# A hybrid encoder block: a fourth g_attn unit in the state-space rounds, side work at fixed places in an attention block

## The chip, the cores and the metric

The kernel runs on one core of one Trainium2 chip. The core has TensorE (PE, matmuls), VectorE (DVE), ScalarE (ACT), GpSimd (POOL) and SyncE (SP), which here only issues DMAs. Each engine executes its own instructions in the order in which the program issues them and waits on semaphores for the others. The metric is the device time of one execution in microseconds (us).

## The reference

One layer of an encoder block on a sequence of 1024 tokens of width 1024, in float32:

```python
proj = h @ w_in                     # h = RMSNorm(x) * (1 + scale) + shift
q, k, v, z_a, u, z_s, g_a, g_s = jnp.split(proj, IN_OFFSETS, axis=-1)
o = diff_attention(rope(q), rope(k), v, lam)          # 4 heads, two softmax maps each
o = rmsnorm(o, g_subln) * (1.0 - lam_init)            # per head
attn_branch = (o.reshape(b, s, ATTN_WIDTH) * jax.nn.silu(z_a)) @ w_up_attn
y = s5_forward(u) + s5_backward(u) + d_skip * u       # 32 groups, complex diagonal state
y = jax.nn.gelu(y); y = y * jax.nn.sigmoid(y @ w_glu + b_glu)
ssm_branch = (y * jax.nn.silu(z_s)) @ w_up_ssm
merged = jax.nn.sigmoid(g_a) * attn_branch + jax.nn.sigmoid(g_s) * ssm_branch
out = rmsnorm(x + gate * (merged @ w_out), g_final)
```

The projection's 128 column blocks that matter here: eight blocks of g_attn (g_a), whose tanh is kept in DRAM until the merge.

## The kernel before

Every float32 product is made of three matmuls: a weight is split into a high part `wh` (ACT copies it into a rounded type) and a low part `wl` (DVE or POOL subtracts), the other operand likewise, and high times high, high times low and low times high are summed in PSUM. A *unit* (`unit`, lines 209 to 222) is 128 columns of the projection: two halves of 512 tokens, eight steps of three matmuls each, so 16 steps. Weights come in the order of the list `plan`; `w_ahead` (called in the first step of a unit) loads and splits those of the next unit or two. `w_state["eng"]` says whether DVE or POOL makes the low parts: DVE in the state-space rounds, POOL in attention.

The program is a hand-made order. A *main* generator issues the work of a stage and yields amounts of budget; `drive` takes that budget from a *fill* generator, whose units yield 0.66 per step. So the constants `YF, YA, YB, YC` (state-space rounds, `ssm_main`) and `FA, FB, LA, LB` (attention, `s3_main`) say how many fill steps stand between the pieces of main work on PE.

- State-space rounds (`ssm_main`): eight rounds; in each DVE does the stages a, rot, c, s (scans) and d. Four yields of YA, one of YB and one of YC a round. The fill is the rest of u, z_ssm, z_attn, g_ssm and the first `GA1 = 3` units of g_attn.
- `s2_main`: what is left of that fill, then the gated linear unit and the up-projection of the state-space branch (`unit_pair`, evacuated by `up_ev` on DVE as tile `pt`).
- Attention (`s3_main`): 34 blocks g, eight per head. A block issues `qk` (scores; DVE takes the maximum, ACT the exponential), `mix` of the block before (the DVE operation on tile `e`), `pv` in odd blocks, half of the fill, the other half, `transpose_w` of the block before (PE transposes of `e`; ACT and DVE split them into `wth` and `wtl`), and the late fill. `spot(0)`, `spot(1)` and `spot(2)` are three places in it for side work. The fill is q, k and v of heads 1 to 3 and the remaining units of g_attn.
- Side work: the rope of q and k (`turn`: a shuffle on DVE and three operations on POOL; `cut`: the split, ACT and POOL) waits in the queue `pend` and `with_pend` pops one entry at every second fill step, wherever in a block that is. `make_v` and, right behind it, `o_turn` (PE transposes of the last head's output) stand in block 2 of a head; the steps of `o_norm` (the head's RMSNorm) stand at every spot after that, one each.
- `s3_tail`: the turn and the norm of head 3, reloads of the normed heads, splits into `oh` and `ol`, under what is left of the fill; then the up-projection of attention, the merge and the output projection.

Of the kernel before, what the change touches and what calls it, by code (L numbers as in the profile page):

```python
# [9 lines left out]
F32 = mybir.dt.float32  # L10
# [56 lines left out]
def tile_hybrid_block(  # L67
# [63 lines left out]
    w0 = w_in[0]  # L131
    OQ, OK, OV, OZA, OU, OZS, OGA, OGS = 0, 512, 1024, 1536, 2048, 2560, 3072, 4096

    GA1 = 3
    YF, YA, YB, YC, YL = 10.5, 2.6, 4.6, 2.8, 3.0
    NPE = (3, 4, 2, 1, 0, 0, 0, 1)
    WN = 16
    plan = []
# [39 lines left out]
    def w_split():  # L178
        i = w_state["split"]
        if i >= len(plan):  # L180
            return
        r = w_raw.pop(i)
        h = pp.tile([P, 8 * P], F32R, tag="wh", bufs=2, name="wh")
        l = pp.tile([P, 8 * P], F32R, tag="wl", bufs=2, name="wl")
        split(h, l, r, w_state["eng"])
        k = plan[i][2]
        w_hl[i] = tuple(t[:].rearrange("p (k n) -> p k n", k=k) for t in (h, l))
        w_state["split"] += 1
# [17 lines left out]
        while w_state["load"] <= min(i + 1, len(plan) - 1):  # L206
            w_load()

    def unit(c0, K, rh, rl, evac, pool=None, w=None, off=0, ahead=True):
        wh, wl = w or w_get(c0)  # L210
        for hf in range(2):
            ps = (pool or ps_mm).tile([P, 512], F32, tag="mm", name="mm")
            sl = slice(hf * 512, hf * 512 + 512)
            n = 0
            for k in range(K):
                for a, r in ((wh, rh), (wh, rl), (wl, rh)):
                    PE.matmul(out=ps, lhsT=a[:, k, off:off + P], rhs=r[:, k, sl], start=(n == 0), stop=(n == 3 * K - 1))  # L217
                    n += 1
                if ahead and hf == 0 and k == 0:
                    w_ahead()  # L220
                yield 0.66
            evac(hf, sl, ps)

    def unit_pair(c0, rh, rl, evacs, pool=None):
        w = w_get(c0)
        for b in range(2):
            yield from unit(c0, 4, rh, rl, evacs[b], pool, w, b * P, b == 0)

    def run_all(g):
        for _ in g:  # L230
# [964 lines left out]
    def s2_main():  # L1195
        ps2 = tc.alloc_tile_pool(name="ps_s2", bufs=1, space=PSUM, side="right")
        yp = tc.alloc_tile_pool(name="yp", bufs=1, side="right")
        y2h = yp.tile([P, 4, S], F32R, name="y2h")
        y2l = yp.tile([P, 4, S], F32R, name="y2l")
        gts = {}  # L1200

        def load_g(m):
            if m < 8:
                gts[m] = yp.tile([P, S], F32, tag="gt", bufs=3, name="gt")
                SP.dma_start(out=gts[m], in_=gsd[m])

        yq = tc.alloc_tile_pool(name="yq", bufs=1, side="right")
        yh = yq.tile([P, 4, S], F32R, name="yh")
        yl = yq.tile([P, 4, S], F32R, name="yl")
        zts = {}  # L1210

        def load_z(n):
            if n < 4:
                zts[n] = yq.tile([P, S], F32, tag="zt", bufs=2, name="zt")
                SP.dma_start(out=zts[n], in_=zsd[n])

        co = yp.tile([P, T * 8], F32, name="cos")
        sn = yp.tile([P, T * 8], F32, name="sin")
        yp.tile([P, 120], F32, name="pad")
        G.tensor_copy(out=co, in_=rt["co"])  # L1220
        G.tensor_copy(out=sn, in_=rt["sn"])
        rt.update(co=co, sn=sn)
        t = yq.tile([P, S], F32, name="yt")
        for r in range(2):
            SP.dma_start(out=t[64 * r:64 * r + 64], in_=yd[3 * P + 64 * r:3 * P + 64 * r + 64, :])
        yield 2.0
        for b in range(3):
            split(yh[:, b], yl[:, b], ye[:, b])
            yield 1.5
        load_z(0)  # L1230
        load_z(1)
        act(t[0:64], t[0:64], AF.Gelu_apprx_tanh)
        split(yh[:, 3], yl[:, 3], t)
        yield 1000.0

        def glu_ev(n):
            def ev(hf, sl, ps):
                zt = zts[n]
                sg = yq.tile([P, 512], F32, tag="sg", bufs=2, name="sg")
                mul(zt[:, sl], zt[:, sl], (ye[:, n] if n < 3 else t)[:, sl])  # L1240
                act(sg, ps, AF.Sigmoid, bias=cols[:, CBG + n:CBG + n + 1])
                mul(sg, sg, zt[:, sl])
                split(y2h[:, n, sl], y2l[:, n, sl], sg)
                if hf == 1:
                    load_z(n + 2)
            return ev

        for n in range(0, 4, 2):
            for q in unit_pair(n * P, yh, yl, [glu_ev(n), glu_ev(n + 1)]):
                yield q  # L1250
            if n == 0:
                for m in range(3):
                    load_g(m)
        yq.release()
        yep.release()
        p2 = tc.alloc_tile_pool(name="p2", bufs=1, side="left")
        cosT = p2.tile([P, S], F32, name="cosT")
        sinT = p2.tile([P, S], F32, name="sinT")
        rt.update(p2=p2, cosT=cosT, sinT=sinT)
        yg = tc.alloc_tile_pool(name="yg", bufs=1, side="right")  # L1260
        prep = side_prep(yg, ps2)
        pts = {}
        def up_ev(m):
            def ev(hf, sl, ps):
                gt = gts[m]
                if hf == 0:
                    pts[m] = yg.tile([P, S], F32, tag="pt", bufs=2, name="pt")
                stt(pts[m][:, sl], gt[:, sl], 1.0, ps, ALU.add, ALU.mult)
                if hf == 1:
                    A.dma_start(out=pad[m], in_=pts[m])  # L1270
                    load_g(m + 3)
            return ev

        for m in range(0, 8, 2):
            for q in unit_pair(m * P, y2h, y2l, [up_ev(m), up_ev(m + 1)]):
                next(prep, None)
                yield q
        run_all(prep)
        yg.release()
        yp.release()  # L1280
        ps2.release()
# [17 lines left out]

    def skip():  # L1300
        pass

    def with_pend(g, every):
        for n, q in enumerate(g):
# [4 lines left out]
    def rope_unit(c0, scale, h, finish):  # L1309
        t = {}  # L1310

        def ev(hf, sl, ps):
# [21 lines left out]
                if h == 0:  # L1334
                    finish(hi, lo, sl)

            pend.extend([turn, skip, skip, cut])
            if hf == 1 and h > 0:
                pend.append(lambda: finish(t["h"], lo, slice(0, S)))
        yield from unit(c0, 8, hh, hl, ev)  # L1340

    def prep_q(h):
# [67 lines left out]
    def qk(g):  # L1410
        h, i = divmod(g, 8)
        H = heads[h]
        if i == 0:
            flush()
            H["o"] = po.tile([P, S], F32, tag="o", bufs=2, name="o")
            H["zr"] = po.tile([P, 8, 2], F32, tag="zr", bufs=2, name="zr")
        tok = slice(i * P, i * P + P)
# [64 lines left out]
    def o_norm(h, e=G, big=None):  # L1482
        H = heads[h]
        on, zr, o = H["on"], H["zr"], H["o"]
        ss = po.tile([P, 8], F32, tag="oss", name="oss")
        z2 = po.tile([P, 8], F32, tag="wm", bufs=2, name="z2")
        for hf in range(2):
            sl = slice(hf * 512, hf * 512 + 512)
            if big is None:
                jk = p3.tile([P, 512], F32, tag="tb", name="sq")  # L1490
            else:
                jk = big[:, sl]
            act(jk, o[:, sl], AF.Square)
            yield
            V.tensor_reduce(out=ss[:, 4 * hf:4 * hf + 4], in_=jk.rearrange("p (t e) -> p t e", t=4) if big is not None
                            else jk[:].rearrange("p (t e) -> p t e", t=4), axis=AX.X, op=ALU.add)
        mul(z2, zr[:, :, 0], zr[:, :, 0])
        mul(ss, ss, z2)
        yield
        res = []  # L1500
        for n, _ in enumerate(rsqrt_gen(po, ss, 8, 1.0 / P, "o", res)):
            if n % 3 == 2:
                yield
        rs = res[0]
        mul(rs, rs, zr[:, :, 0])
        mul(on, on, bc(rs[:], 2, [P, 8, P]), e)
        yield
# [15 lines left out]
    def s3_main():  # L1523
# [4 lines left out]
        NG = 32  # L1528
        gens = {}

        def spot(s, g):
            h, i = divmod(g, 8)
            if g < 8:
                return
            if (i, s) == (2, 0) and h < 4:
                make_v(h)
            if (i, s) == (2, 1) and h < 4:
                o_turn(h - 1)
                gens[h] = o_norm(h - 1)
            elif h in gens and next(gens[h], gens) is gens:  # L1540
                gens.pop(h)
            if (i, s) == (5, 0):
                load_za(h - 1)
            if (i, s) == (6, 0):
                assert h not in gens
                SP.dma_start(out=ofd[h - 1], in_=o_back(h - 1))

        for g in range(NG + 2):
            fa, fb = (FA, FB) if g < 24 else (LA, LB)
# [15 lines left out]
            spot(2, g)  # L1565
            yield fb / 2

    FA, FB, FD = 3.1, 1.0, 1.0
    LA, LB = 2.45, 1.0
    fill3 = with_pend(s3_fill(), 2)  # L1570
    drive(s3_main(), fill3)
    p3.release()
    p2.release()
# [12 lines left out]
    def s3_tail():  # L1586
# [5 lines left out]
        for h in range(3):  # L1592
            ofl.append(op.tile([P, S], F32, tag="sg", bufs=3, name="ofl"))
            SP.dma_start(out=ofl[h], in_=ofd[h])
        next(norm)
        yield 3.0
        run_all(norm)
# [195 lines left out]
```

## Time and profile before

| | us |
|---|---|
| median of 3 runs (lowest to highest) | 912.46 (911.06 to 912.81) |
| the profiled execution | 911.19 |
| its span, first to last instruction | 909.3 |
| PE busy in the span | 873.0 |
| rounds with their fill | about 108 to 340 |
| attention | 459 to 754 |
| norm tail | 754 to 769.5 |

The times of the rows come from the one profiled execution, counted from the start of its span. A matmul's end is modelled and matmuls overlap, so the idle time of PE is taken from stretches and from the starts of matmuls, not from the sum of durations.

### The profile page before, as it was taken

The page shows a single profiled execution, that of the slowest core. Times are in us where ns is not written, and L with a number is a line of the kernel's source. Part 1 is how long each engine was busy: PE and PEld are TensorE (multiplying, and loading weights), DVE is VectorE, ACT ScalarE, POOL GpSimd, SP SyncE. Part 2 cuts the span into 40 slices and gives each one's busy share as a digit, 9 for nine tenths or more (in the row PEclk, how much of TensorE's full clock was granted, in tenths as well). Part 3 has the DMA queues.
Part 4 walks back from the last instruction along what each step waited for, and adds up shares of the span by engine and source line. Part 5 has one row for each costly group of instructions (what it writes and reads, how often), then busy time and mean ns, then how long its engine had stood idle before and what let it go on. Part 6 is the DMA issues. An engine that isn't in the chain of part 4 may idle for free.

```text
span 909.3 us, 12201 instructions
## 1 busy us (share of the span) xinstructions
PE 873.0 (96%) x4528; PEld 732.6 (81%) x4528; DVE 673.3 (74%) x1264; ACT 366.1 (40%) x610; POOL 134.5 (15%) x115
## 2 busy tenths in 40 slices
PE   5999999999999899999999999898999999999996
PEld 4878888888888788787878887787788888887886
DVE  5986999899999976674657767875866756573465
ACT  6754442132222236301246556455555544232222
POOL 1001000000000001000025434423511111350000
PEclk9899899999999999999999999999999999999999
DMA  9936133333243446595433313132232224848022
GB/s 296 307 83 186 52 112 110 101 98 118 85 126 107 125 139 196 207 327 185 123 98 81 91 38 81 64 95 63 70 105 58 81 94 140 333 176 312 12 88 98
DMA packets 107117, 119.56 MB, mean 131 GB/s; under 512 B 7716, under 2 KB 87825, under 8 KB 107059
## 3 DMA queue, kind: packets, MB, share of 16 engines
q1 hardware_dynamic: 105268, 114.08, 40.5%
q10 hardware_dynamic: 1614, 4.51, 1.2%
q8 instruction: 36, 0.59, 0.3%
q0 software_dynamic: 176, 0.20, 0.1%
q14 instruction: 23, 0.18, 0.1%
HBM read 78.46 MB, written 27.73 MB: 117 GB/s over the span
## 4 chain that ended last, share of the span: by engine, by line
PE 41%; DVE 7%; ACT 3%; DMA 2%; issue 2%; POOL 2%; SPq 0%; ACTq 0%; DVEq 0%; POOLq 0%
PE mm L217 19%; PE op L1712 9%; PE pv L1468 4%; PE tp L1457 3%; PE sc L1427 3%; PE sc L1426 2%; DVE nm L1428 2%; POOL pta L78 1%; DVE e L96 1%; ACT e L99 1%; DVE wtl L78 1%; DMA wor<-in_w_out_dram 1%; DMA pad<-pt 1%; ACT mh L99 1%; DMA pta<-pad 1%
## 5 line engine op out<-in xcount | busy, mean ns | idle before, releaser
L217 PE MATMUL mm<-hh,wh 128*128 128x512 f32 x592 | 239.1, 404 | 0.0
L217 PE MATMUL mm<-hh,wl 128*128 128x512 f32 x592 | 232.6, 393 | 2.9 <-DVE wl L78 2.8
L217 PE MATMUL mm<-hl,wh 128*128 128x512 f32 x592 | 232.6, 393 | 0.0
L217 PEld LDWEIGHTS mm<-hh,wl 128*128 128x128 f32 x592 | 112.1, 189 | 28.2 <-DVE wl L78 4.1
L217 PEld LDWEIGHTS mm<-hh,wh 128*128 128x128 f32 x592 | 112.3, 190 | 22.4 <-issue 1.7
L217 PEld LDWEIGHTS mm<-hl,wh 128*128 128x128 f32 x592 | 112.5, 190 | 20.4
L99 ACT ACTIVATE e<-sc,nm 128x1024 f32<-128x1024 f32 x64 | 71.2, 1115 | 77.1 <-DVE nm L1428 77.0
L1428 DVE TENSOR_REDUCE nm<-sc 128x1 f32<-128x1024 f32 x64 | 75.3, 1218 | 14.2 <-PE sc L1427 13.1
L78 DVE TENSOR_TENSOR wtl<-tp,wth 128x512 fp32r<-128x512 f32 x64 | 41.2, 686 | 60.0 <-ACT wth L99 59.9
L99 ACT ACTIVATE wh<-wr 128x1024 fp32r<-128x1024 f32 x49 | 51.7, 1056 | 62.0 <-DMA wr<-in_w_in_dram 24.2
L99 ACT ACTIVATE side<-mm 128x512 f32<-128x512 f32 x48 | 28.7, 598 | 112.8 <-PE mm L217 78.5
L78 POOL TENSOR_TENSOR wl<-wr,wh 128x1024 fp32r<-128x1024 f32 x14 | 34.7, 2477 | 207.2 <-ACT wh L99 207.0
L78 DVE TENSOR_TENSOR wl<-wr,wh 128x1024 fp32r<-128x1024 f32 x35 | 42.9, 1227 | 29.2 <-ACT wh L99 29.0
L1712 PE MATMUL op<-woh,ml 128*128 128x512 f32 (+1 forms) x136 | 51.3, 377 | 1.1 <-DVE ml L78 1.1
L1712 PE MATMUL op<-wol,mh 128*128 128x512 f32 (+1 forms) x136 | 51.2, 377 | 0.0
L1712 PE MATMUL op<-woh,mh 128*128 128x512 f32 (+1 forms) x136 | 51.2, 377 | 0.0
L99 ACT ACTIVATE wth<-tp 128x512 fp32r<-128x512 f32 x64 | 34.8, 596 | 40.1 <-PE tp L1457 40.1
L1426 PE MATMUL sc<-kk,qq 128*128 128x512 f32 x128 | 49.9, 390 | 0.0
L1427 PE MATMUL sc<-kk,qb 128*128 128x512 f32 x128 | 49.9, 390 | 0.0
L96 DVE SCALAR_TENSOR_TENSOR e<-e,wm 128x1024 f32<-128x1024 f32 x32 | 45.3, 1415 | 1.1
L1468 PE MATMUL pv<-wth,vh 128*128 128x256 f32 x128 | 36.5, 285 | 2.7 <-DVE wtl L78 2.7
L1457 PE MATMUL tp<-cst,e 128*128 128x128 f32 x256 | 33.3, 273 | 5.8 <-DVE nry L78 2.4
(365 smaller groups left out, 1693.1 us busy)
## 6 DMA issues: line engine op xcount, KB each, us to landing
wr<-in_w_in_dram SPq DMA_DIRECT2D x40, 512.0 KB
wa<-in_w_ada_dram SPq DMA_DIRECT2D x16, 512.0 KB
x<-in_x_dram SPq DMA_DIRECT2D x8, 512.0 KB
gsd<-side SPq DMA_DIRECT2D x8, 512.0 KB
gad<-side SPq DMA_DIRECT2D x8, 512.0 KB
gt<-gsd SPq DMA_DIRECT2D x8, 512.0 KB
wg<-in_w_ada_dram SPq DMA_DIRECT2D x8, 512.0 KB
pad<-pt ACTq DMA_DIRECT2D x8, 512.0 KB
```

Of the source, the lines that this page charges most:

```text
L78: (e or V).tensor_tensor(out=o, in0=a, in1=b, op=op)
L96: V.scalar_tensor_tensor(out=o, in0=a, scalar=s, in1=b, op0=op0, op1=op1)
L99: A.activation(out=o, in_=i, func=f, **kw)
L217: PE.matmul(out=ps, lhsT=a[:, k, off:off + P], rhs=r[:, k, sl], start=(n == 0), stop=(n == 3 * K - 1))
L1426: PE.matmul(out=sc[:, sl], lhsT=H["qq"][:, cc, tok], rhs=H["kk"][:, cc, sl], start=True, stop=False)
L1427: PE.matmul(out=sc[:, sl], lhsT=qb_t[g // 2][:, cc, tb], rhs=H["kk"][:, cc, sl], start=False, stop=True)
L1428: V.tensor_reduce(out=nm[:, cc:cc + 1], in_=sc, axis=AX.X, op=ALU.max, negate=True)
L1457: PE.transpose(ps[:, k, :], e[:, kt * P:kt * P + P], ident)
L1468: PE.matmul(out=ps[:, 0:256], lhsT=a[:, kt, :], rhs=r[:, kt, :], start=(n == 0), stop=(n == 23))
L1712: PE.matmul(out=ps[:, 0:n], lhsT=a[:, k, tok], rhs=r[:, k, lo:lo + n], start=(i == 0), stop=(i == 23))
```

## The change

It puts a fourth unit of g_attn into the rounds (`GA1`), with larger Y constants; raises `FA` from 3.1 to 3.2; cuts POOL's subtraction for a weight split into two halves; lets `unit_pair` of the state-space up-projection call `w_ahead` at the second half's first step; and gives each kind of side work a place: turns at spot 0 of a block, one each; the last cut of a head at spot 2 from block 5 on; `o_turn` at block 3, spot 1; the nine steps of `o_norm` at the places of `STEPS`; the transposes back and the store of a normed head at block 0 of the head after next.

```diff
-    GA1 = 3
-    YF, YA, YB, YC, YL = 10.5, 2.6, 4.6, 2.8, 3.0
+    GA1 = 4
+    YF, YA, YB, YC, YL = 12.0, 2.75, 4.8, 3.2, 3.0
...
-        split(h, l, r, w_state["eng"])
+        act(h, r, AF.Copy)
+        if w_state["eng"] is G:
+            for j in range(0, 8 * P, 512):
+                sub(l[:, j:j + 512], r[:, j:j + 512], f32(h[:, j:j + 512]), G)
+        else:
+            sub(l, r, f32(h))
...
-                if ahead and hf == 0 and k == 0:
+                if (hf, k) == ahead:
                     w_ahead()
...
-            for q in unit_pair(m * P, y2h, y2l, [up_ev(m), up_ev(m + 1)]):
+            for q in unit_pair(m * P, y2h, y2l, [up_ev(m), up_ev(m + 1)], ahead=(1, 0)):
...
+    def pop_turn():
+        while pend:
+            kind, fn = pend.popleft()
+            fn()
+            if kind == "turn":
+                break
+
+    def pop_cut():
+        if pend and pend[0][0] == "cut":
+            pend.popleft()[1]()
...
-            pend.extend([turn, skip, skip, cut])
-            if hf == 1 and h > 0:
-                pend.append(lambda: finish(t["h"], lo, slice(0, S)))
+            def cut_all():
+                cut()
+                if hf == 1:
+                    finish(t["h"], lo, slice(0, S))
+
+            pend.extend([turn, skip, skip, cut] if h == 0 else [("turn", turn), ("cut", cut_all)])
...
         if i == 0:
-            flush()
+            while pend:
+                pop_turn()
...
             act(jk, o[:, sl], AF.Square)
             yield
+            if hf == 1:
+                z2 = po.tile([P, 8], F32, tag="wm", bufs=2, name="z2")
             V.tensor_reduce(out=ss[:, 4 * hf:4 * hf + 4], in_=jk.rearrange("p (t e) -> p t e", t=4) if big is not None
                             else jk[:].rearrange("p (t e) -> p t e", t=4), axis=AX.X, op=ALU.add)
+            if hf == 0:
+                yield
...
+        STEPS = ((3, 2), (4, 0), (4, 2), (5, 0), (5, 1), (6, 0), (6, 1), (7, 0), (7, 1))
+
         def spot(s, g):
             h, i = divmod(g, 8)
-            if g < 8:
+            if 1 <= h < 4 and (i, s) in STEPS:
+                next(gens[h], None)
+            if s == 0:
+                pop_turn()
+            if s == 2 and i >= 5:
+                pop_cut()
+            if (i, s) == (0, 0) and h >= 2:
+                SP.dma_start(out=ofd[h - 2], in_=o_back(h - 2))
+            if not 1 <= h < 4:
                 return
-            if (i, s) == (2, 0) and h < 4:
+            if (i, s) == (2, 0):
                 make_v(h)
-            if (i, s) == (2, 1) and h < 4:
+            if (i, s) == (3, 1):
                 o_turn(h - 1)
                 gens[h] = o_norm(h - 1)
-            elif h in gens and next(gens[h], gens) is gens:
-                gens.pop(h)
-            if (i, s) == (5, 0):
+            if (i, s) == (7, 0):
                 load_za(h - 1)
-            if (i, s) == (6, 0):
-                assert h not in gens
-                SP.dma_start(out=ofd[h - 1], in_=o_back(h - 1))
...
-    FA, FB, FD = 3.1, 1.0, 1.0
+    FA, FB, FD = 3.2, 1.0, 1.0
     LA, LB = 2.45, 1.0
-    fill3 = with_pend(s3_fill(), 2)
+    fill3 = s3_fill()
...
         next(norm)
+        next(norm)
         yield 3.0
```

## Rows read from the trace of the kernel before

**Rows 1.** Page, part 1: busy us (share of the span) xinstructions
```profile
PE 873.0 (96%) x4528; PEld 732.6 (81%) x4528; DVE 673.3 (74%) x1264; ACT 366.1 (40%) x610; POOL 134.5 (15%) x115
```

**Rows 2.** Chain of waits in order of time: start us, us, what
```profile
754.07 12.94 PE mm L217 x57
```

**Rows 3.** Waits, PE: engine line waited for: us in total, times, longest us
```profile
PE tp L1479 <- DVE vl L78: 3.2, 3, 1.1
PE mm L217 <- DVE wl L78: 2.8, 1, 2.8
PE pv L1468 <- DVE wtl L78: 2.7, 3, 2.0
PE tp L1457 <- DVE nry L78: 2.4, 2, 1.7
PE tp L1457 <- DVE nrt L78: 2.2, 2, 1.3
PE mm L217 <- DVE pt L96: 1.3, 1, 1.3
```

**Rows 4.** Stretches: length, busy us of PE, PEld, DVE, ACT, POOL, granted clock, DMA
```profile
203.40:228.20 24.80, 24.80 (x147) 21.21 (x147) 24.13 (x36) 6.78 (x13) 0.20 (x2) 1.00 0.42 125
302.80:327.00 24.20, 21.38 (x121) 17.80 (x120) 23.17 (x33) 3.85 (x9) 0.20 (x2) 0.93 0.29 86
459.00:541.00 82.00, 80.62 (x438) 69.26 (x439) 56.23 (x76) 46.07 (x81) 34.12 (x23) 1.00 0.29 75
541.00:616.00 75.00, 70.51 (x398) 60.06 (x397) 56.46 (x85) 39.70 (x72) 30.79 (x21) 1.00 0.29 78
616.00:691.00 75.00, 70.23 (x396) 59.67 (x395) 52.97 (x84) 39.43 (x72) 24.33 (x16) 1.00 0.26 71
691.00:754.00 63.00, 61.66 (x360) 53.20 (x360) 41.10 (x70) 32.71 (x59) 9.13 (x4) 1.00 0.29 94
754.00:769.50 15.50, 15.50 (x74) 12.93 (x73) 11.96 (x23) 7.36 (x11) 3.40 (x1) 1.00 0.33 113
...
313.00:316.00 3.00, 3.00 (x9) 2.33 (x8) 2.93 (x7) 0.00 (x0) 0.00 (x0) 0.50 0.00 0
```

**Rows 5.** Timeline, the late weight split: start us, us, engine line op tiles
```profile
300.02 1.06 ACT L99 ACTIVATE wh<-wr 128x1024 fp32r<-128x1024 f32 x1 [6.11 <-DMA wr<-in_w_in_dram]
...
310.79 1.23 DVE L78 TENSOR_TENSOR wl<-wr,wh 128x1024 fp32r<-128x1024 f32 x1
```

**Rows 6.** Timeline of DVE at the first state-space up-projection
```profile
380.60 1.23 DVE L78 TENSOR_TENSOR wl<-wr,wh 128x1024 fp32r<-128x1024 f32 x1 [0.26 <-ACT wh L99]
381.74 1.28 DVE L96 SCALAR_TENSOR_TENSOR pt<-gt,mm 128x512 f32<-128x512 f32 x2
```

**Rows 7.** Timeline of DVE and POOL in two attention blocks
```profile
566.27 2.40 DVE L96 SCALAR_TENSOR_TENSOR e<-e,wm 128x1024 f32<-128x1024 f32 x1
...
566.30 1.29 POOL L78 TENSOR_TENSOR rq<-rq,rs 128x512 f32<-128x512 f32 x1
568.58 2.43 POOL L78 TENSOR_TENSOR wl<-wr,wh 128x1024 fp32r<-128x1024 f32 x1 [0.99 <-ACT wh L99]
...
603.93 1.28 DVE L96 SCALAR_TENSOR_TENSOR e<-e,wm 128x1024 f32<-128x1024 f32 x1
```

**Rows 8.** Timeline of PE, DVE and ACT in the norm tail
```profile
753.03 1.03 PE L1479 MATMUL tp<-cst,o 128*128 128x128 f32 x8
...
759.74 1.23 DVE L78 TENSOR_TENSOR o<-o,nry 128x1024 f32<-128x1024 f32 x1
760.88 5.69 DVE L78 TENSOR_TENSOR ol<-ofl,oh 128x1024 fp32r<-128x1024 f32 x3
767.48 1.41 DVE L96 SCALAR_TENSOR_TENSOR of<-tp,cols,of 128x512 f32<-128x512 f32 x2 [0.91 <-PE tp L1516]
...
768.92 1.06 ACT L99 ACTIVATE oh<-of 128x1024 fp32r<-128x1024 f32 x1 [4.63 <-DVE of L96]
770.02 1.23 DVE L78 TENSOR_TENSOR ol<-of,oh 128x1024 fp32r<-128x1024 f32 x1 [1.13 <-ACT oh L99]
```

More of the change, by code (lines that the diff above doesn't have):

```diff
@@ L207, in w_ahead, with unit @@
             w_load()
-    def unit(c0, K, rh, rl, evac, pool=None, w=None, off=0, ahead=True):
+    def unit(c0, K, rh, rl, evac, pool=None, w=None, off=0, ahead=(0, 0)):
         wh, wl = w or w_get(c0)
@@ L222, in unit, with unit_pair @@
             evac(hf, sl, ps)
-    def unit_pair(c0, rh, rl, evacs, pool=None):
+    def unit_pair(c0, rh, rl, evacs, pool=None, ahead=(0, 0)):
         w = w_get(c0)
         for b in range(2):
-            yield from unit(c0, 4, rh, rl, evacs[b], pool, w, b * P, b == 0)
+            yield from unit(c0, 4, rh, rl, evacs[b], pool, w, b * P, None if b else ahead)
     def run_all(g):
@@ L1485, in o_norm @@
         ss = po.tile([P, 8], F32, tag="oss", name="oss")
-        z2 = po.tile([P, 8], F32, tag="wm", bufs=2, name="z2")
         for hf in range(2):
```

## Prediction

> **What bounds the kernel now.** I read the page first: TensorE (PE) is busy 96% of the span, VectorE (DVE) 74%, GpSimd (POOL) 15% [rows 1]. PE executes in order, so the time is PE's work plus PE's gaps, and an edit is worth the gaps that it closes or opens. PE's work is not changed by this edit: the same matmuls run. 57 matmuls of 512 columns take 12.94 us in the chain of waits [rows 2], 0.227 us each; one unit of 48 is 10.9 us, one fill step (three matmuls) 0.68 us.
>
> Next the list of waits, PE's own [rows 3]: six entries carry the inner gaps. The stretches say where they lie [rows 4]. In attention (459 to 754 us) PE is busy 80.62 of 82, 70.51 of 75, 70.23 of 75 and 61.66 of 63 us: 12.0 us of gaps, 9.3 of them in the two middle rows, the blocks of heads 1 and 2, where rope work for the next head and the norm of the last head meet. In a state-space round (203.4 to 228.2) PE is busy 24.80 of 24.80 and DVE 24.13: both are full, and DVE is about to be the later one. At the end of the rounds it is: between 302.8 and 327 PE is idle for 2.8 us and the granted clock is 0.93, another 0.07 x 24.2 = 1.7 us. In the norm tail (754 to 769.5) PE is busy throughout.
>
> **The change, part by part.**
>
> *One unit moves (GA1 = 4, the Y values).* The rounds' budget grows by 1.5 + 8 x (4 x 0.15 + 0.2 + 0.4) = 11.1, that is 16.8 steps of 0.66, and the unit has 16. So the rounds take the whole unit, +10.9 us of PE there, and attention loses 10.9. Net of work: nothing. What the rounds gain is slack for DVE: 1.2 of budget more a round, 1.24 us of PE time, while DVE gets one weight split more in all. At 308.9 the matmul that waited needed a weight low part whose high part ScalarE (ACT) had ready at 301.08; DVE started it at 310.79 [rows 5], 9.7 us late, behind a backlog. With 0.7 us a round DVE was nearly level; with 1.9 us over eight rounds the backlog goes. I take the whole gap and the clock dip behind it away: **-4.5 us**. Bounds: 0 (another split falls behind the scans) to -4.5. The fill that is left after the last round, which covers the prologue of the gate, shrinks by at most one step; the stretch from 327 to 354 has no gap and I cost this at nothing; without that cover it would be up to 0.7.
>
> *Split of the up-projection's weights one half later (ahead = (1, 0)).* At 380.73 PE waits for DVE to clear a PSUM half. DVE did the weight split (380.60, 1.23 us) ahead of the clearing operation pt [rows 6]. In the new order pt comes first and the wait of 1.3 us [rows 3] goes: **-1.3**. The split is now 2.7 us later in a pair that lasts 10.9 us, so its reader is not late; bounds -1.3 to 0.
>
> *Side work at fixed places in attention.* (a) The turn of the head's output (o_turn) moves from right behind make_v to the next block. In all three heads PE waited 1.1 us for vl, whose PSUM buffers it needed [rows 3]: 3.2 us, gone; at the new place the buffers were cleared a block before. (b) The norm steps and the rope turns: PE's transposes wait for nrt and nry (4.6 us) and pv for wtl (2.7 us) [rows 3]. The rows show why. The mixing operation e takes 1.28 us at 603.93 but 2.40 at 566.27, where POOL runs a rope addition of 1.29 from 566.30 [rows 7]: the longer by what POOL took. So a DVE operation with two SBUF inputs stands still beside POOL. In the new order the rope work starts right behind e in each block (spot 0) and has most of a block (295 us / 34 = 8.7) until the next e: cut 1.3 + turn 3 x 1.3 = 5.2 us of POOL [rows 7], so it is over by then unless a weight split (2.43 us [rows 7], now two halves) falls in. And only one norm step stands in front of a transpose instead of a varying number. Of the 12.0 us I leave 2.5: the first block's wait and the last pv's, which nothing here touches (about 1.2), and one or two collisions of 1.3. **-9.5**, bounds -11 (only the untouched waits stay) and -4 (only the 3.2 of o_turn and one more go). Neither (a) nor (b) adds PE work.
> The Trainium skill (GPSIMD Engine Reference, section 1, Specifications) says that GpSimd's SBUF interfaces are shared with VectorE and contend with its two-input instructions; the rows above agree, and by that rule alone a POOL chain that runs into the next e costs again what it cost before, which is the second rival.
>
> *Moved DMAs and queues.* The store of a normed head moves from block 6 to block 0 of the head after, the load of za from block 5 to 7. On SyncE's queue the weight loads and query copies behind the store wait for the same few DVE operations as before, and have a unit's time (10.9 us) of lead; for head 2 the store falls into block 32, some 5 us before its reload is issued, which waits for pv's end in any case. I cost them at nothing; a load that is late would cost 1 to 2 us. The halved POOL split adds 0.1 us per split on an engine that is busy 15%.
>
> *Fill 4.2.* Counting steps by the budget rule: 24 blocks and 10 late blocks used 202 of 224 steps before, and 22 were left for the tail; now they use 205 of 208, and **3 are left**. This is the price of the change. The norm of head 3 ran under 19 steps of fill. Its chain [rows 8]: from the turn at 753.03 to the multiply by the norm at 759.74 is 6.7 us; then 1.23 for it, 3 x 1.23 for the low parts of heads 0 to 2 (they took 5.69 because POOL was splitting beside them; that split is now earlier), 1.41 for `of`, 1.06 for the high part and 1.23 for the low part: 15.3 us. PE has in that time two turns of 1.03, nine fill matmuls (2.04) and ten of the up-projection that need not wait for head 3 (2.27): 6.4. So PE idles **+9.0 us**, where it had no gap. Bounds: 7 (part of the small operations overlap) to 10.5 (the slow low parts return).
>
> *The clock behind that gap.* After the 2.8 us gap at 309 the granted clock was 0.50 from 313 to 316 [rows 4], half of full, that is 1.2 instead of 2.4 GHz: 1.5 us lost. The new gap is longer. I take **+1.5**, bounds 0 (it comes back before the up-projection runs densely) and 3 (twice as long low).
> The Trainium skill (TensorE: Matmul & The Clock Gate, "Why this matters for your kernels") warns against idle gaps in the middle of a kernel because the clock falls; it speaks against this part, and row and rule agree on the sign.
>
> **Sum.** -4.5 - 1.3 - 9.5 + 9.0 + 1.5 = -4.8. The profiled execution took 911.19 (span 909.3 and 1.9 around it), the median of the runs is 912.46, so the profile is 1.3 us under the median. From the profile 906.4, from the median 907.7; I say **907.0**.
>
> **The rivals.**
> 1. *Forecast*, 904.5 to 910: chance 0.52.
> 2. *Slower: the POOL chain still runs into e.* Each of the 12 blocks with a rope turn loses 1.1 us (2.40 - 1.28), so the 12.0 us of gaps stay, while the tail pays its 10.5. 911.19 - 4.5 - 1.3 + 10.5 = 915.9, from the median 917. It decides as soon as fewer than 4.7 of the 12.0 us go. For it: ACT must make the cut's high part behind two exponentials before POOL can begin, so the chain ends late in the block. Against it: the blocks from 459 to 541 already had such turns and lost only 1.4 us. Chance 0.13.
> 3. *The waits only half go* (about 6 of 12.0): 911.19 - 4.5 - 1.3 - 6 + 10.5 = 909.9, from the median 911: 0.15, at the edge of the 0.2% bound, so I split it evenly between faster and same.
> 4. *The rounds stay bound by DVE*, so that the unit is moved but the gap at 309 stays or moves: 906.4 + 4.5 = 910.9, from the median 912. DVE is over 97% busy in a round, but the added fill is three to four times what it needs: 0.08.
> 5. *The tail is cheaper* (7 us, no clock loss) and attention loses only 1 us: 911.19 - 4.5 - 1.3 - 11 + 7 = 901.4, from the median 902.7: 0.12.
>
> **How the numbers follow.** Faster by over 0.2% (1.8 us, about what measurement can tell from no change) means under 910.6: the forecast, rival 5 and half of rival 3, 0.71. Within it: rival 4, half of 3 and a little of 2, 0.17. Slower: 0.12. The range 902.5 to 913.5 takes in the bounds of the tail and of the attention waits and leaves out most of rival 2 and the best end of rival 5.
>
> **What would show it.** In the profile after: rounds of about 26.0 us with PE full, DVE under 24.5, and no gap for wl at their end, granted clock 1.00; no wait for pt at the first up-projection of the state-space branch; no waits for vl in o_turn, and 1 to 4 us of gaps over all attention blocks; between the last pv and the first up-projection of attention a gap of 8 to 10 us on PE that ends on DVE's ol, with a granted clock near 0.5 in or behind it; every e near 1.28 us. The prediction is wrong in its first term if that tail gap is under 6 us, and in its main gain if e still shows 2.4 in many blocks.

## The result, and the profile after

| | us |
|---|---|
| before, median of 4 runs (lowest to highest) | 912.62 (911.06 to 912.81) |
| after, median of 4 runs (lowest to highest) | 901.87 (899.86 to 902.09) |
| ratio, with its 95% interval | 0.9885 (0.9871 to 0.9900) |
| the profiled execution of after; its span | 901.95; 899.7 |

The changed kernel is faster, by 10.7 us where 5.5 were forecast. The time lies 0.6 us under the lower end of the range.

The waits of PE in the profile after (engine, line, what it waited for: us in total, times, longest us), those of the lead-in left out, are the counterpart of [rows 3]:

```profile
PE tp L1539 <- DVE o L78: 4.9, 1, 4.9
PE mm L222 <- DVE of L96: 2.8, 1, 2.8
PE tp L1477 <- DVE nrt L78: 1.2, 1, 1.2
PE tp L1539 <- POOL wl L78: 0.7, 1, 0.7
```

Of the six entries of [rows 3], five are gone (vl, wl, wtl, nry, pt) and nrt went from 2.2 to 1.2 us. New are the two on `o` and `of`, 7.7 us, both in the norm of head 3, and one of 0.7 us on POOL's `wl`.

The stretches of the profile after (length, busy us of PE, PEld, DVE, ACT, POOL, granted clock, DMA share, GB/s) answer to [rows 4]: a round, the last rounds, the four parts of attention, the norm tail, and the half of the tail behind its first gap:

```profile
208.00:234.20 26.20, 26.20 (x153) 22.38 (x153) 24.60 (x37) 7.14 (x13) 0.20 (x2) 1.00 0.41 123
312.00:338.00 26.00, 26.00 (x150) 22.10 (x149) 19.90 (x31) 8.09 (x14) 0.20 (x2) 1.00 0.50 146
...
463.00:545.00 82.00, 81.52 (x442) 70.05 (x443) 54.51 (x75) 45.57 (x79) 33.14 (x27) 1.00 0.30 78
545.00:620.00 75.00, 73.77 (x418) 63.73 (x418) 57.26 (x89) 41.97 (x76) 32.92 (x26) 1.00 0.29 78
620.00:695.00 75.00, 75.00 (x427) 65.01 (x426) 55.97 (x91) 44.74 (x80) 26.86 (x21) 1.00 0.31 85
695.00:745.00 50.00, 49.30 (x292) 42.68 (x291) 34.54 (x60) 25.35 (x45) 6.92 (x5) 1.00 0.21 70
745.00:764.00 19.00, 11.30 (x49) 9.06 (x48) 12.01 (x25) 8.17 (x11) 0.00 (x0) 0.73 0.70 252
...
756.00:764.00 8.00, 5.21 (x17) 4.08 (x16) 6.39 (x7) 2.00 (x2) 0.00 (x0) 0.53 0.80 270
```

PE is full through the rounds, DVE has 1.6 us to spare in one, and the end of the rounds has neither its gap nor its clock of 0.93. Attention shows 2.4 us of idle PE (0.48 + 1.23 + 0 + 0.70) where it had 12.0. In the tail PE is busy 11.3 of 19 us, and the granted clock falls to 0.53, near the lower of its two levels (1.2 of 2.4 GHz).

**PE's lost time by stage.** Idle time between modelled ends is not the whole of what PE loses. The next table goes by the starts of matmuls alone: between each two successive starts, what is over the 0.227 us of a 512 column matmul (or the usual step of a shorter one), added up by stage. These sums are worked out from all matmul starts of each profile, and with the number of matmuls in a stage they give its length. For the profile after they come to 9.7 us less than before; its span is 9.6 us shorter (909.3 to 899.7).

| lost time, us | before | after | a_ga3 | b_unit | g_waste | w2 |
|---|---|---|---|---|---|---|
| lead-in, up to the first stage c | 19.0 | 18.6 | 20.1 | 18.4 | 18.4 | 20.1 |
| rounds | 5.6 | 0.6 | 5.8 | 0.6 | 0.6 | 0.6 |
| up-projection of the state-space branch | 4.4 | 2.3 | 2.3 | 4.4 | 2.3 | 2.8 |
| attention blocks, to the last pv | 18.8 | 7.4 | 7.0 | 18.9 | 7.0 | 6.8 |
| norm tail | 0.2 | 9.1 | 1.5 | 7.1 | 1.4 | 1.5 |
| up-projection of attention | -0.1 | 1.7 | 0.1 | 2.6 | 0.1 | 0.1 |
| output projection and end | 1.3 | -0.1 | 1.6 | -0.1 | -0.1 | 1.5 |

(The other columns belong to the experiments; g_waste has in its tail 34 extra matmuls, 7.7 us of work, that are not lost time.)

### The profile page after: what moved, and what is told of

It reads as the page before. It is cut to its first block, busy times and chain, and to the rows that moved or that the text cites. A ratio compares the mean times of both kernels' runs of the same rounds, so it can differ in the third digit from the quotient of the medians.

```text
span 899.7 us, 12212 instructions
## 1 busy us (share of the span) xinstructions
PE 870.5 (97%) x4528; PEld 734.0 (82%) x4528; DVE 667.8 (74%) x1265; ACT 366.3 (41%) x610; POOL 132.9 (15%) x127
## 5 line engine op out<-in xcount | busy, mean ns | idle before, releaser
L222 PE MATMUL mm<-hh,wh 128*128 128x512 f32 x592 | 238.2, 402 | 0.0
L222 PE MATMUL mm<-hl,wh 128*128 128x512 f32 x592 | 232.0, 392 | 0.0
L222 PE MATMUL mm<-hh,wl 128*128 128x512 f32 x592 | 231.7, 391 | 0.0
L222 PEld LDWEIGHTS mm<-hh,wl 128*128 128x128 f32 x592 | 111.7, 189 | 24.3 <-DVE wl L78 0.5
L222 PEld LDWEIGHTS mm<-hh,wh 128*128 128x128 f32 x592 | 111.9, 189 | 22.4 <-issue 1.7
L222 PEld LDWEIGHTS mm<-hl,wh 128*128 128x128 f32 x592 | 112.0, 189 | 20.2
L78 DVE TENSOR_TENSOR wtl<-tp,wth 128x512 fp32r<-128x512 f32 x64 | 41.2, 686 | 55.7 <-ACT wth L99 55.7
L78 DVE TENSOR_TENSOR wl<-wr,wh 128x1024 fp32r<-128x1024 f32 x36 | 44.9, 1250 | 27.8 <-ACT wh L99 27.7
L78 POOL TENSOR_TENSOR wl<-wr,wh 128x512 fp32r<-128x512 f32 x26 | 33.0, 1292 | 139.9 <-ACT wh L99 139.8
L96 DVE SCALAR_TENSOR_TENSOR e<-e,wm 128x1024 f32<-128x1024 f32 x32 | 42.1, 1314 | 1.1
L1488 PE MATMUL pv<-wth,vl 128*128 128x256 f32 x128 | 36.2, 283 | 0.0
```

Source lines behind the costliest of these rows:

```text
L78: (e or V).tensor_tensor(out=o, in0=a, in1=b, op=op)
L96: V.scalar_tensor_tensor(out=o, in0=a, scalar=s, in1=b, op0=op0, op1=op1)
L1488: PE.matmul(out=ps[:, 0:256], lhsT=a[:, kt, :], rhs=r[:, kt, :], start=(n == 0), stop=(n == 23))
```

## The experiments

The theory to be tested is the prediction's mechanisms with larger sizes: each edit closes the gap that it was said to close, and the moved unit is paid for in the tail. The rivals are named with each kernel. Three kernels undo one part each (a_ga3, c_ahead, d_oturn), three undo or change one kind of side work (e_rope, n_steps, f_whole), one makes a single part alone (b_unit), one fills the tail (g_waste), and two look for a better balance (w1, w2). Every ratio below is to runs of the kernel before that belong to it; their medians lie between 911.07 and 912.62 us, so a difference of up to 1.5 us between the medians of two changed kernels can be drift. What a stage gained or lost is therefore read from the starts of matmuls, from one profile of each kernel.

**a_ga3: the changed kernel without the moved unit.** Is the unit a gain or a price?

```diff
-    GA1 = 4
-    YF, YA, YB, YC, YL = 12.0, 2.75, 4.8, 3.2, 3.0
+    GA1 = 3
+    YF, YA, YB, YC, YL = 10.5, 2.6, 4.6, 2.8, 3.0
```

> The changed kernel with GA1 = 3 and the old Y values: the one unit goes back to attention, all else as changed. Theory (each gap is its own price): the DVE gap at the end of the rounds and its clock dip come back (+5.0 us by starts of matmuls), 19 fill steps are again left for the norm tail so its gap and its clock loss go (-10.6), and the wait for ml ahead of the output projection returns (+1.4): about 897.7, faster than the changed kernel by 4. Rival (the slack in the rounds is what the gain rests on, the tail's gap is hidden by loads that come late anyway): 901.9 + 5 = 907.

Measured: 898.81 us (897.95 to 900.30), ratio to before 0.9849 (0.9832 to 0.9865). It is 3.1 us faster than the changed kernel, where 4 were expected; its lead-in loses 1.5 us more (see the last section). The unit is a net loss there, and the whole gain comes from what a_ga3 keeps: the side work, the split of the up-projection's weights and FA 3.2. Of PE's waits in its profile these carry the reading:

```profile
PE mm L222 <- DVE wl L78: 2.8, 1, 2.8
PE mm L222 <- DVE of L96: 1.2, 1, 1.2
PE op L1741 <- DVE ml L78: 1.1, 1, 1.1
```

The gap at the end of the rounds is back (`wl`), the tail loses 1.2 instead of 7.7, and a wait on `ml` in the output projection is back, which the prediction had not counted.

**b_unit: the kernel before, with the moved unit alone** (the same two lines, the other way).

> The kernel before with GA1 = 4 and the new Y values alone: side work and FA as before. 202 of 208 steps used in attention, 6 left for the tail. Theory: rounds -5.0, norm tail with 6 instead of 3 steps +8.6, wait for ml -1.4, attention as before: 912.6 + 2.2 = 914.8. Rival (one unit less in attention also relieves its blocks): under 908.

Measured: 914.25 us (912.15 to 915.54), ratio 1.0020 (1.0011 to 1.0030): slower, as expected. In PE's waits every entry of attention is within 0.1 us of what it was in [rows 3]; `wl` has gone and two of the tail have come:

```profile
PE tp L1479 <- DVE vl L78: 3.2, 3, 1.1
PE tp L1516 <- DVE o L78: 2.9, 1, 2.9
PE mm L217 <- DVE of L96: 2.8, 1, 2.8
PE pv L1468 <- DVE wtl L78: 2.7, 3, 2.0
```

So the waits of attention have nothing to do with the unit, and the unit costs 2 to 3 us net in both surroundings.

**c_ahead: the weight split of the up-projection back at its old place.**

```diff
-            for q in unit_pair(m * P, y2h, y2l, [up_ev(m), up_ev(m + 1)], ahead=(1, 0)):
+            for q in unit_pair(m * P, y2h, y2l, [up_ev(m), up_ev(m + 1)]):
```

> The changed kernel with the state-space up-projection's weight split back at the first half. Theory: the wait for pt returns, +1.3, and if the second wait there (for gacc, 0.4) is its work too, +2.1: 903.2 to 904.0. Rival (those two waits went for another reason): 901.9.

Measured: 903.97 us (901.64 to 904.58), ratio 0.9904 (0.9889 to 0.9919): 2.1 us more than the changed kernel. The entry for `pt` is back in PE's waits at its old length (`PE mm L222 <- DVE pt L96: 1.3, 1, 1.3`). By the starts of matmuls that gap is 1.51 us, and a second one of 0.41 us, in front of the sums on `gacc`, came back with it: the part is worth 2.1, not 1.3. In the profile after, DVE's order is what the prediction said, the clearing operation first and the split behind it:

```profile
386.29 0.69 DVE L96 SCALAR_TENSOR_TENSOR pt<-gt,mm 128x512 f32<-128x512 f32 x1
386.90 1.22 DVE L78 TENSOR_TENSOR wl<-wr,wh 128x1024 fp32r<-128x1024 f32 x1
```

**d_oturn: the turn of the head's output back right behind make_v.**

```diff
-            if (i, s) == (3, 1):
+            if (i, s) == (2, 1):
                 o_turn(h - 1)
+            if (i, s) == (3, 1):
                 gens[h] = o_norm(h - 1)
```

> The changed kernel with o_turn back behind make_v (block 2, spot 1), the norm steps as changed. Theory (buffers that vl must clear): three gaps of 1.2 us on PE, each ended by DVE's vl, 905.5. Rival (the wait for vl came from DVE being late with side work, which now stands elsewhere): no such gaps, 901.9.

Measured: 908.15 us (905.80 to 910.79), ratio 0.9962 (0.9948 to 0.9975). The three waits are back and longer than before, `PE tp L1499 <- DVE vl L78: 4.9, 3, 1.7`, where [rows 3] has 3.2 in all; by starts they are 1.74, 1.74 and 1.90 us. In the profile DVE itself waits 0.63 us for ACT's high part at that place, which it did not before:

```profile
549.06 1.29 DVE L78 TENSOR_TENSOR vl<-tp,vh 128x512 fp32r<-128x512 f32 x2 [0.63 <-ACT vh L99]
```

The mechanism is the predicted one. The size is not: the lost time of attention rises by 5.4 us, which is the three gaps. The profiled execution rises by 3.9 only (901.95 to 905.80), because its lead-in is 2.1 us shorter than that of after (see the last section); its up-projection of attention, behind the tail's gap, loses 1.2 us more. The medians differ by 6.3; no profile shows where the other 0.9 lie in those runs.

**e_rope: rope work popped at every second fill step again**, the rest as changed.

```diff
-            pend.extend([turn, skip, skip, cut] if h == 0 else [("turn", turn), ("cut", cut_all)])
+            pend.extend([turn, skip, skip, cut if h == 0 else cut_all])
...
-            while pend:
-                pop_turn()
+            flush()
...
-            if s == 0:
-                pop_turn()
-            if s == 2 and i >= 5:
-                pop_cut()
...
-    fill3 = s3_fill()
+    fill3 = with_pend(s3_fill(), 2)
```

> The changed kernel with the rope queue popped at every second fill step again; norm steps and o_turn at their new places. Theory (rope operations of POOL that run into the mixing operation e and into the squares of the norm): waits on e, wtl and the norm's squares come back, 3 to 6 us: 905 to 908, with several e of about 2.4 us. Rival (the norm steps made those waits, the rope turns are harmless, as in head 0's blocks before): 901.9 within 1.

Measured: 904.38 us (902.36 to 905.34), ratio 0.9911 (0.9886 to 0.9936): 2.5 us more than the changed kernel, just below the expected range. The collisions with POOL are back in the operation `e`; of its group (count, busy us, mean ns, idle before) the profile of e_rope has

```profile
L96 DVE SCALAR_TENSOR_TENSOR e<-e,wm 128x1024 f32<-128x1024 f32 x32 | 46.2, 1443 | 1.1
```

where after has

```profile
L96 DVE SCALAR_TENSOR_TENSOR e<-e,wm 128x1024 f32<-128x1024 f32 x32 | 42.1, 1314 | 1.1
```

so 4.1 us of collisions come back on DVE: five of the 32 operations take 2.26 to 2.40 us, each beside a rope operation of POOL, where the changed kernel has one long one. PE loses 3.2 us more in attention (10.6 instead of 7.4), but most of that is not behind `e`. What PE waits for in attention begins with

```profile
PE tp L1476 <- ACT o L99: 1.7, 2, 0.8
PE tp L1498 <- ACT o L99: 1.1, 1, 1.1
PE tp L1476 <- DVE e L96: 1.0, 3, 0.5
```

The three gaps on ACT's `o` end at 563.0, 582.8 and 655.0 us and are 3.2 us long by starts. Shortly before each, ACT stands idle for over 5 us until POOL's rope chain lets it go on:

```profile
559.87 0.63 ACT L99 ACTIVATE rh<-rq 128x512 fp32r<-128x512 f32 x1 [5.10 <-POOL rq L78]
579.67 0.63 ACT L99 ACTIVATE sq<-o 128x512 f32<-128x512 f32 x1 [5.56 <-POOL rq L78]
651.33 0.63 ACT L99 ACTIVATE rh<-rq 128x512 fp32r<-128x512 f32 x1 [5.03 <-POOL rq L78]
```

ACT executes in order, so the exponentials and `o` behind these come late. In the changed kernel no wait of ACT for POOL in attention is over 3.4 us.

**n_steps: one step of the norm at every spot again (from block 3, spot 2)**, the rest as changed.

```diff
-            if 1 <= h < 4 and (i, s) in STEPS:
+            if h in gens:
                 next(gens[h], None)
```

> The changed kernel with the norm's nine steps at every spot from block 3 spot 2 on instead of the places of the list; rope turns as changed. Theory (rope and POOL make the waits): at most 1 us more, 902 to 903. Rival (norm steps close together hold DVE in front of the transposes): 2 to 4 us more, waits on nrt and nry at PE's transposes, 904 to 906.

Measured: 905.84 us (904.96 to 908.06), ratio 0.9934 (0.9908 to 0.9960). The time is the rival's, but its mechanism is another. One gap carries it (`PE pv L1488 <- DVE wtl L78: 3.8, 1, 3.8`), and DVE is not busy with norm steps in front of it; ACT waits:

```profile
572.72 0.63 ACT L99 ACTIVATE sq<-o 128x512 f32<-128x512 f32 x1 [5.38 <-POOL rq L78]
573.25 0.58 ACT L99 ACTIVATE rq<-mm 128x512 f32<-128x512 f32 x1
573.73 1.05 ACT L99 ACTIVATE wh<-wr 128x1024 fp32r<-128x1024 f32 x1
574.68 1.07 ACT L99 ACTIVATE wth<-tp 128x512 fp32r<-128x512 f32 x2
```

The square of the norm writes a temporary that shares its one buffer (tag `tb`) with the rope's `rs`. Issued in the middle of POOL's rope chain it waits 5.38 us for the buffer, on an engine that executes in order, with the `wth` that PE needs three operations behind it. In the changed kernel the same square stands a block later; it waits 2.99 us for the same chain, but PE has no gap there. So `STEPS` is worth 4.0 us by the medians, for a reason that the prediction did not have: it spoke of DVE alone. By starts attention loses 5.0 us more than in the changed kernel: 4.0 are this gap, and right behind it the granted clock is 0.50 from 577.2 to 580.6.

**f_whole: POOL's subtraction in one operation again.**

```diff
-            for j in range(0, 8 * P, 512):
-                sub(l[:, j:j + 512], r[:, j:j + 512], f32(h[:, j:j + 512]), G)
+            sub(l, r, f32(h), G)
```

> The changed kernel with GpSimd's low parts of the weight splits in attention whole again (one operation of 128x1024, 2.43 us in the kernel before) instead of two halves of 1.29 us. Theory: the halves matter little, because what they can hold up is the mixing operation e, and in the changed kernel only the blocks in which a split meets e are long at all (e mean 1.31 us over 32, that is 0.9 us in total above 1.285). Whole operations can make such a block longer by at most 1.1 us, in one to three blocks: 901.9 to 903.5, e mean 1.31 to 1.38 us, attention's gaps 7.4 to 9 us. Rival: the halving is what gives DVE its turn between two GpSimd operations, and whole ones bring back a good part of the waits of attention: 904 to 907, e mean over 1.40 us.

Measured: 901.60 us (900.63 to 902.91), ratio 0.9894 (0.9872 to 0.9916): the same as the changed kernel, and `e` has even a mean of 1285 ns, no collision left. The halving is worth nothing that these runs can tell.

**g_waste: the tail's gaps filled with matmuls whose result is not used.** How much of the tail is the clock?

```diff
+    def waste(n):
+        ps = ps_mm.tile([P, 512], F32, tag="mm", name="mm")
+        for j in range(n):
+            PE.matmul(out=ps, lhsT=hh[:, j % 8, 0:P], rhs=hh[:, j % 8, 0:512], start=(j == 0), stop=(j == n - 1))
...
+        waste(22)
         of = o_back(3)
+        waste(12)
```

> The changed kernel with 34 throwaway matmuls in the norm tail (22 ahead of the transposes back of head 3, 12 behind them; nobody reads their sum), 7.7 us of PE work in a gap of about 8. Theory (the gap costs twice: as idle time and by the clock that falls in it): the granted clock stays at 1.00, the up-projection behind it loses its 1.7 us and the transposes 0.9: 901.9 - 2.6 = 899.3. Rival (the clock dip has another cause, or the matmuls delay the chain): 902 or more.

Measured: 900.15 us (897.95 to 900.93), ratio 0.9864 (0.9838 to 0.9889): 1.7 us less than the changed kernel, with more work. The tail on PE in its profile, and its stretch to be held against the 756 to 764 of after:

```profile
749.89 5.15 PE L1617 MATMUL mm<-hh 128*128 128x512 f32 x22
754.97 1.06 PE L1539 MATMUL tp<-cst,o 128*128 128x128 f32 x8
755.78 3.02 PE L1617 MATMUL mm<-hh 128*128 128x512 f32 x12
759.69 0.47 PE L222 MATMUL mm<-oh,wh 128*128 128x512 f32 x1 [0.88 <-DVE of L96]
```

```profile
756.00:764.00 8.00, 7.12 (x32) 5.46 (x31) 6.50 (x7) 2.01 (x2) 0.23 (x1) 1.00 0.86 312
```

The clock stays at 1.00 where it was 0.53. The up-projection still begins at 759.7, 0.5 us earlier, and 0.4 of that was gained ahead of the tail: the transposes are 0.9 us shorter, but the norm's chain on DVE sets the start, so of the 2.6 us expected these 0.9 did not come. The 1.6 us that the table shows in the next stage are gone. So the clock's part of the price was about 1.7 us in this pair, and the rest is idle time that only useful work could earn back. In the other profiles with this gap (b_unit, c_ahead, d_oturn, e_rope, n_steps, f_whole) the stage behind it loses 1.7 to 2.8 us by starts.

**w1 and w2: the unit back in attention, with the rounds' Y values in between.** If the unit costs 3 us, and the gap at the end of the rounds is one of pace, a little more fill in the rounds should close that gap without emptying the tail. w1 has fill 4.1 (FA 3.1), w2 has 4.2.

```diff
-    GA1 = 4
-    YF, YA, YB, YC, YL = 12.0, 2.75, 4.8, 3.2, 3.0
+    GA1 = 3
+    YF, YA, YB, YC, YL = 10.5, 2.6, 4.8, 3.0, 3.0
...
-    FA, FB, FD = 3.2, 1.0, 1.0
+    FA, FB, FD = 3.1, 1.0, 1.0
```

(the last pair in w1 alone)

> The changed kernel with GA1 = 3 and Y values 10.5, 2.6, 4.8, 3.0: the fourth unit stays in attention and covers the norm tail again (FA 3.1, 22 steps left), and the rounds take 3.2 of budget (5 steps) more from the fill behind them. Theory (the gap of 3.0 us at the end of the rounds closes with some 2.6 us more of slack by then, 15 steps still cover the gate's prologue): 898.8 - 4 - 1.3 = 893.5 to 895. Rival (DVE's backlog needs the whole unit): the gap of about 3 us and the dip stay, 897.5 to 899.

Measured for w1: 897.66 us (897.12 to 898.10), ratio 0.9838 (0.9812 to 0.9864): the rival's time, but not for its reason. The rounds' gap went (1.0 us of lost time), while attention lost 11.2 where a_ga3 lost 7.0.

> The changed kernel with the fourth unit back in attention (GA1 = 3), the Y values 10.5, 2.6, 4.8, 3.0, 3.0 and the fill left at 4.2. It differs from the earlier kernel w1 in the fill alone (4.1 there) and from a_ga3 in two Y values alone. If the gaps are additive over the stages, it has w1's rounds (1.0 us of gaps where a_ga3 had 5.8), a_ga3's attention (7.0 where w1 had 11.2) and a_ga3's tail (1.5 where w1 had 0.2): w1's 897.66 less 4.2 and plus 1.3 is 894.8 us, from a_ga3's 898.81 less 4.8 is 894.0; 893.5 to 896. Rival: the places of the weight splits in attention have moved with the Y values, and w1's four gaps of 0.8 to 1.7 us come from that and not from the fill; then they stay and the tail's 1.3 comes on top: 898 to 899.5.

Measured for w2: 894.95 us (893.12 to 895.45), ratio 0.9819 (0.9801 to 0.9838): the fastest of all, under the changed kernel by 6.9 us in the medians and by 6.0 in the ratios to before, and the sum over the stages holds. Its stretches: the four parts of attention and the norm tail.

```profile
454.00:536.00 82.00, 81.45 (x442) 69.96 (x443) 54.51 (x75) 45.54 (x80) 33.07 (x26) 1.00 0.29 74
536.00:611.00 75.00, 74.12 (x422) 64.06 (x421) 57.09 (x89) 42.15 (x76) 33.20 (x26) 1.00 0.29 78
611.00:686.00 75.00, 75.00 (x426) 65.00 (x425) 55.95 (x91) 44.52 (x80) 26.65 (x21) 1.00 0.30 85
686.00:735.70 49.70, 49.27 (x294) 42.74 (x293) 34.58 (x60) 25.35 (x45) 6.91 (x5) 1.00 0.25 80
735.70:754.00 18.30, 17.14 (x86) 14.22 (x85) 11.94 (x23) 7.74 (x12) 2.55 (x2) 1.00 0.42 145
```

PE is idle 1.9 us in attention and 1.2 in the tail, and the clock is 1.00 in all five stretches. w1 and w2 differ in FA alone: with 4.2 attention loses 6.8 us instead of 11.2 and the tail 1.5 instead of 0.2. So 4.4 us of attention hang on the fill, and the rival for w2 falls; how a tenth of budget a block does that is not shown.

## Why the prediction was wrong

The direction and the sign of every counted term were right. The prediction failed in the **sizes of the gains**, which all came out too small: most of all in the term of attention (-9.5, measured -11.4), and in a term that it put at nothing, the output projection (-1.4). It also gave the gain of attention to the side work alone. The cost came out at its size, in part by luck. The sum was -4.8 us and the profiles differ by 9.7:

| step of the prediction | forecast | by the starts of matmuls |
|---|---|---|
| rounds: gap and clock | -4.5 | -5.0 |
| up-projection's weight split | -1.3 | -2.1 |
| attention: side work, and FA 3.2 with it | -9.5 | -11.4 |
| tail gap and clock behind it | +10.5 | +10.6 |
| output projection | not counted | -1.4 |
| lead-in | not counted | -0.4 |

- **Attention, the term that was mis-sized most.** In idle time the forecast was right almost to the tenth: 12.0 us in the stretches of [rows 4] became 2.4, and 2.5 were to be left. But idle time of a stretch is counted from the modelled end of a matmul (0.39 us after its start), while the next could have started after 0.227. Each gap is thus 0.16 us longer than it looks (the waits on vl, 1.1 each in [rows 3], are 1.22 by starts). Before has twelve gaps of over 0.25 us in attention, 13.9 us by starts, and after has four, 3.3; that is 10.6 of the 11.4. The other 0.8 lies in smaller differences that were not followed up. For this reason the bound of -11 was also too tight.
- **Inside attention, where the gain comes from.** The sum counted fill 4.2 as a price in the tail alone. By w1 and w2 it is also a gain of 4.4 us in attention, and at FA 3.1 the side work takes attention from 18.8 to 11.2, 7.6 us and not 9.5 (both with three units in the rounds; the kernel before with FA 3.2 was not run). Undone singly at FA 3.2, the turn of the output costs 5.4 by starts where 3.2 were put, rope at free places 3.2, the norm's steps at every spot 5.0, and the whole split of POOL nothing. These overlap and need not add up.
- **Inside attention, the mechanism.** For the turn it is the predicted one. The waits on nrt, nry and wtl (7.3 us in [rows 3]) were put down to `e` beside POOL and to norm steps of DVE. Two of them follow an `e` of 2.40 us: PE's gaps that end at 568.82 and 580.44, 3.0 us idle in all. The longest, 2.0 us on wtl before 631.94, does not: ahead of it ACT stands idle for POOL's rope, with `wth` next in its order.

```profile
630.05 0.63 ACT L99 ACTIVATE rh<-rq 128x512 fp32r<-128x512 f32 x1 [5.38 <-POOL rq L78]
```

  That is the wait that e_rope brings back three times and n_steps once. The prediction named ACT's place in the rope's cut in rival 2, but not that ACT's own later work, and PE behind it, would wait.
- **The up-projection.** The wait on `pt` went as said; the second gap, on `gacc`, is in no row that was read, and went too (c_ahead: 2.1 us).
- **The output projection** was costed at nothing because the change does not touch it. In the kernel before the last store of the g_attn rows is issued at 770.60 and the first reload at 771.02; DVE waits 2.5 us for a reload in the up-projection (`sga`, filled from `gad`) and is late for `ml` at the end. With the fourth unit out of the tail the last store is issued at 751.19 and the first reload at 756.46 (the first two lines are of before, the others of after):

```profile
770.60 0.32 SPq L1118 DMA_DIRECT2D gad<-side  x1
771.02 0.37 SPq L1582 DMA_DIRECT2D sga<-gad  x1
...
751.19 0.32 SPq L1123 DMA_DIRECT2D gad<-side  x1
756.46 0.32 SPq L1610 DMA_DIRECT2D sga<-gad  x1
```

  In the profiles of before, a_ga3, w1 and w2 (three units in the rounds) both waits are there, `sga` with 2.3 to 2.5 us; in those of after and b_unit neither is. That the moved unit removes them is shown by that; that the late store alone does it is argued from the two issue times.
- **The tail**, with the stage behind it, came to 10.6 us for 10.5, but that is luck: two slips in it cancel. PE's matmuls of the up-projection did not run ten early: the first waits for `of`, not for `ol` as was said, and starts at 760.17. And its start does not wait for head 3's high and low parts, which the sum had put ahead of it: 1.06 + 1.23 us too much, 2.27 too little.

```profile
754.08 1.23 DVE L78 TENSOR_TENSOR o<-o,nry 128x1024 f32<-128x1024 f32 x1
755.22 3.49 DVE L78 TENSOR_TENSOR ol<-ofl,oh 128x1024 fp32r<-128x1024 f32 x3
755.45 1.94 PE L1539 MATMUL tp<-cst,o 128*128 128x128 f32 x8 [4.92 <-DVE o L78]
760.17 0.77 PE L222 MATMUL mm<-oh,wh 128*128 128x512 f32 x1 [2.79 <-DVE of L96]
```

  The low parts took 3.49 us instead of the 5.69 of [rows 8], as forecast (3 x 1.23), and the transposes 1.94 us at the low clock against 1.06 in g_waste at the full one.
- **The clock** was put at 1.5 us, with bounds of 0 and 3, and is 1.7 by g_waste (1.7 to 2.8 over the profiles with this gap). The Trainium skill (TensorE: Matmul & The Clock Gate, "Why this matters for your kernels") warns of idle gaps for this; the stretch with 0.53, and 1.00 once the gap is filled, agree.
- **The base.** 907.0 lay between the sum from the profile (906.4) and from the median (907.7). The terms are worth 4.9 us more than forecast, the profile gives 0.6 less than 907.0, and the time outside the span is 0.4 longer in the profile after (2.25 against 1.89): that is the 5.1 between 907.0 and 901.9.
- **The rivals.** Rival 5 came nearest in time (901.4 from the profile, 902.7 from the median) and in attention (-11), but its tail of 7 us without a clock loss is not the one measured. Rivals 2 and 3 are excluded by the 2.4 us that are left of 12.0 and by `e` (mean 1.314 us, 1.415 before), rival 4 by the full rounds.

## What to carry to other kernels

Size a gap on an engine whose instructions overlap by the distance of successive starts, not by idle time. An edit that closes a gap should be followed one stage further, to the stores and reloads whose time it shifts, even where nothing is edited. Look at what an engine off the critical path waits for: here ACT stood behind POOL's rope, and PE paid for it. And where a unit of filler is moved out of a late stage, count what the last stage needs before it is taken: here a pace in between (w2) kept the gain of the rounds without the price of the tail, 6 to 7 us better than the change.

## What the runs showed of the hardware

- **Tiny VectorE operations can be slow beside GpSimd.** Two norm steps of 128x8 took 1.2 to 1.3 us beside a rope operation of POOL in the profile after; the step ahead of them, with POOL idle, took 0.16:

```profile
580.88 0.16 DVE L93 TENSOR_SCALAR rqv<-oss 128x8 f32<-128x8 f32 x1
581.08 1.31 DVE L91 TENSOR_SCALAR nri<-rqv 128x8 int32<-128x8 int32 x1
582.42 1.21 DVE L93 TENSOR_SCALAR nry<-nri 128x8 int32<-128x8 int32 x1
...
581.07 1.29 POOL L78 TENSOR_TENSOR rs<-rs,sinT 128x512 f32<-128x512 f32 x1 [0.96 <-DVE rqv L93]
582.32 1.29 POOL L78 TENSOR_TENSOR rq<-rq,cosT 128x512 f32<-128x512 f32 x1
```

  These two DVE operations have one tensor input each. The Trainium skill (GPSIMD Engine Reference, section 1, Specifications) names VectorE instructions in a two-port performance mode or with two SBUF inputs as the ones that contend; whether these two run in such a mode no row here shows.
- **A clock dip without a gap, in some profiles only.** Between 95 and 108 us PE is busy throughout, yet the granted clock is 0.75 in the profile after; in that of d_oturn, whose program is the same up to attention, it is 1.00:

```profile
95.00:108.00 13.00, 13.00 (x66) 10.71 (x65) 12.85 (x88) 4.19 (x8) 0.00 (x0) 0.75 0.27 83
```

```profile
95.00:108.00 13.00, 13.00 (x77) 10.90 (x76) 12.84 (x86) 4.08 (x7) 0.00 (x0) 1.00 0.24 68
```

  It costs 2.1 us of lead-in (18.6 against 16.5 us of lost time). In a_ga3 and w2 the clock is 1.00 there, but a wait for `cb` of 2.6 us follows at 123 us. The profile of before has the dip too, and so have six of the eleven since (after, b_unit, c_ahead, e_rope, f_whole, g_waste); what decides it stays open.
